# Compact 32x32 diagonal squares in two mixers, and attention steps that hold both key heads

## The chip, the cores and the metric

The kernel runs on one core of a Trainium2 chip. A core has a matrix engine (PE in the profile, with its weight loads listed apart as PEld), a vector engine (DVE), a scalar engine (ACT), a third elementwise engine (POOL) and a queue engine that issues transfers (SP). The metric is the time of one execution on the device in microseconds, lower is better, as the median of several runs.

## The reference

The program is two transformer-like blocks over 1024 tokens of width 1024, all in float32, one after the other. Three parts of it matter here.

1. Block one, sliding-window attention: 8 query heads of 64 share 2 key heads. Each of 8 query blocks of 128 tokens looks at its own and the preceding block, with a mask and one sink logit per head, as in `probs = softmax(concat([s, sink]))[..., :-1]`.
2. Block one, gated delta rule, 4 heads of 128: per chunk it needs the inverse of a unit lower triangular matrix, `T = triangular_solve(eye + L, eye)`, and then a recurrence over chunks.
3. Block two, an HGRN2 mixer of 6 heads of 128: per chunk the scores are `einsum('bhtk,bhsk,bhtsk->bhts', qb, kb, exp(diff))`, where `diff` is a difference of running sums for every feature k, and so the scores are no plain matrix product. A recurrence over chunks follows here too.

Around these stand projections, two MLPs of width 4096 and norms, which are most of the arithmetic.

## The kernel before, in words

Large products are split: a float32 operand is rounded to a high part and a rest (`split`, L191 and L192), and `acc` (L211 to L213) issues three single-pass matmuls of 128x512 for each tile. Small products run in plain float32. In the trace each plain float32 matmul stands as two matmul records, for instance 128 matmuls as 256 records; below, "record" means one of these.

The mixers work on half the sequence at a time, a tile being 128 partitions by 512 columns, that is four chunks of 128 tokens side by side.

**Attention** (`attn`, L634): one task per query block n and key head kv, 16 tasks. A task goes twice (jj) over two query heads: scores (L649 or L651, 64 rows of the array, those of head kv), mask (L654), maximum, exponential on ACT (L662), division (L668), yield, transposes (L673) and a copy (L675), yield, product with the values (L679, 64 columns of the array). One output tile is kept for the whole task, is copied out once (L682), and then sent by one transfer.

**Delta inverse** (`delta`, L723): X starts as the identity, and level l joins squares of side 2^l into squares of twice the side. Level 0 is elementwise (L776, L777). Levels 1 to 4 issue for each of the four chunks a product of the whole 128x128 L with the odd columns of X (L782), a transpose of X on DVE (L784), a masked copy (L785), a second product per chunk (L789) and a subtraction (L790). Everything that the mask removes was computed too. Levels 5 and 6 (L807, L815) already use blocks of 32 and 64. There are 4 heads by 2 halves, so 8 tasks.

**HGRN scores** (`hgrn`, L1174): the diagonal comes from a full product per chunk (L1181) times the identity; level 0 from one product with ones (L1192); levels 1 to 4 from a product per chunk of all keys with the odd queries (L1196), of which a predicated copy (L1197) keeps the masked part. Levels 5 and 6 use column blocks of 32 and 64 (L1202). There are 6 heads by 2 halves, so 12 tasks.

**What sets the order.** `weave` (L325) steps up to three tasks, one for each lane, in turn. After each round it advances a filler (projections and first output products) at a rate: RA while fewer than FA attention tasks have ended, then RB, then R1 when all have ended; R5 is the HGRN mixer's. Lane 0 takes only the first FA attention tasks, and then delta tasks. Each lane has its own two PSUM tiles (`axps(lane)`). The framework then plans the final order of instructions on each engine from dependencies, tile availability, modelled durations and the order in which the code issued them: an instruction whose inputs the plan has ready can go ahead of one that was issued earlier. On the chip, each engine's queue runs in the planned order.

Of the kernel before, what the change touches and what calls it, by code (L numbers as in the profile page):

```python
# [15 lines left out]
S = 1024  # L16
# [37 lines left out]
RA, RB, R1, R5 = 0.1, 0.2, 0.35, 0.9  # L54
FA, POOL_AT = 10, 2
# [6 lines left out]
def block_kernel(ctx: ExitStack, tc: tile.TileContext, A):  # L62
# [12 lines left out]
    const.tile([128, 64], F32, name="pad")  # L75
# [82 lines left out]
    def mask(l):  # L158

        a = cst("masks")[:, l * 64:(l + 1) * 64].rearrange("p (n b) -> p n b", b=1 << l)  # L160
        return a.unsqueeze(1).to_broadcast([128, 4, 64 >> l, 1 << l])
# [15 lines left out]

    def half4(t, l):

        return t[:, 0:256].rearrange("p (c n b) -> p c n b", c=4, b=1 << l)  # L180
# [339 lines left out]


# [99 lines left out]
    gh, gl = [wba[:, 0:32], wba[:, 32:64]]  # L621
    split(gg, gh, gl)
# [11 lines left out]
    def attn(lane, qr, kr, vT, n, kv):  # L634
# [4 lines left out]
        r = slice(kv * 64, kv * 64 + 64)  # L639
        am = cst("amask")[:, 256 - w:256].unsqueeze(1).to_broadcast([128, 2, w])  # L640
        po = axps(lane)
        for jj in range(2):
            ps = axps(lane)
            p3 = ps[:, :2 * w].rearrange("p (j k) -> p j k", j=2)
            for i in range(2):
                q = qr[2 * jj + i][n // 4][r, cs(n % 4)]
                if n % 4 == 0:
                    for b, m in enumerate(blocks):
                        PE.matmul(p3[:, i, cs(b)], q, kr[m // 4][r, cs(m % 4)], start=True, stop=True)  # L649
                else:  # L650
                    PE.matmul(p3[:, i], q, kr[n // 4][r, (n % 4 - 1) * 128:(n % 4 + 1) * 128], start=True, stop=True)  # L651
            e = td("ab"[jj], lane)
            e3 = e[:, :2 * w].rearrange("p (j k) -> p j k", j=2)
            V.tensor_tensor(e3, p3, am, ALU.add)  # L654
            yield
            m, nm, den, s2 = sm(2, "am"), sm(2, "an"), sm(2, "ad"), sm(2, "as")
            sk = small("sinks", kv * 4 + 2 * jj, 2)
            V.tensor_reduce(m, e3, AX.X, ALU.max)
            V.tensor_tensor(m, m, sk, ALU.max)
            V.tensor_scalar(nm, m, -1.0, None, ALU.mult)  # L660
            for i in range(2):
                SC.activation(e3[:, i], e3[:, i], ACTF.Exp, bias=nm[:, i:i + 1], accum_out=s2[:, i:i + 1])  # L662
            V.tensor_tensor(den, sk, m, ALU.subtract)
# [3 lines left out]
            for i in range(2):  # L667
                V.tensor_scalar(e3[:, i], e3[:, i], den[:, i:i + 1], None, ALU.mult)  # L668
            yield
            pp = axps(lane)  # L670
            for q in range(nb):
                for i in range(2):
                    PE.transpose(pp[:, cs(2 * q + i)], e3[:, i, cs(q)], ident)  # L673
            pT = td("tmp", lane)
            SC.copy(pT[:, :2 * w], pp[:, :2 * w])  # L675
            yield
            for q, m in enumerate(blocks):
                b = (m % 4) * 128 + kv * 64
                PE.matmul(po[r, jj * 256:jj * 256 + 256], vT[m // 4][:, b:b + 64],  # L679
                          pT[:, q * 256:q * 256 + 256], start=(q == 0), stop=(q == nb - 1))  # L680
        f = td("tmp", lane)
        SC.copy(f[r, :], po[r, :])  # L682
        mix["done"].update((n // 4, i) for i in range(4))
        nc.sync.dma_start(
            out=mix["d"][0:512, cs(n)].rearrange("(i q) t -> q i t", q=128)[r],
            in_=f[r, :].rearrange("p (i t) -> p i t", i=4),
        )
# [35 lines left out]
    def delta(lane, j, h, y, z):  # L723
# [49 lines left out]
        X = td("d", lane)  # L773
        Y = td("a", lane)
        G.tensor_copy(g4(X), b4(ident))
        V.tensor_tensor(half4(Y, 0), odd(U, 0, 4), mask(0), ALU.mult)  # L776
        V.tensor_tensor(odd(X, 0, 4), odd(X, 0, 4), half4(Y, 0), ALU.subtract)  # L777
        yield
        for l in range(1, 5):
            py = axps(lane)  # L780
            for c in range(4):
                PE.matmul(py[:, c * 64:c * 64 + 64], L[:, cs(c)], odd(X[:, cs(c)], l), start=True, stop=True)  # L782
            Y, T = td("a", lane), td("b", lane)
            V.transpose(T, X)  # L784
            V.tensor_tensor(half4(Y, l), half4(py, l), mask(l), ALU.mult)  # L785
            yield
            pz = axps(lane)
            for c in range(4):
                PE.matmul(pz[:, c * 64:c * 64 + 64], T[:, cs(c)], Y[:, c * 64:c * 64 + 64], start=True, stop=True)  # L789
            V.tensor_tensor(odd(X, l, 4), odd(X, l, 4), half4(pz, l), ALU.subtract)  # L790
            yield

        for l in range(5, 7):
# [4 lines left out]
            if l == 5:  # L798
                V.transpose(T, X)
# [5 lines left out]
            for c in range(4):  # L805
                for e, o in at:
                    PE.matmul(py[e, c * b:c * b + b], g4(L)[o, c, e], g4(X)[o, c, o], start=True, stop=True)  # L807
# [4 lines left out]
            for c in range(4):  # L812
                m = slice(c * b, c * b + b)
                for e, o in at:
                    PE.matmul(pz[e, m], g4(T)[e, c, e], Y[e, m], start=True, stop=True)  # L815
# [67 lines left out]
    def attn_task(lane, n, kv):  # L883
        yield from attn(lane, *qkv, n, kv)
        over[0] += 1

    def delta_task(lane, jh):

        while over[0] < (FA if lane == 0 else 2 * NC):
# [17 lines left out]
    tasks = [lambda lane, n=n, kv=kv: attn_task(lane, n, kv) for n in range(NC) for kv in range(2)]  # L907
    few = tasks[FA:]
    tasks += [lambda lane, jh=jh: delta_task(lane, jh) for jh in order]
    weave(tasks, fill, lambda: R1 if over[0] == 2 * NC else RB if over[0] >= FA else RA, few)  # L910
# [263 lines left out]
    def hgrn(lane, j, h, q, f, k, vT, g, direct):  # L1174


        sc = tx()[:, 0:H]

        ps = axps(lane)
        for c in range(4):  # L1180
            PE.matmul(ps[:, cs(c)], k[:, cs(c)], q[:, cs(c)], start=True, stop=True)  # L1181
        V.tensor_tensor(g4(sc), g4(ps), b4(ident), ALU.mult)
        yield
        V.tensor_tensor(q, q, f, ALU.mult)
        for l in range(7):
# [235 lines left out]
```

## Time and profile before

| what | value |
|---|---|
| median of 3 runs | 2673.6 us (2668.96 to 2673.8) |
| profiled execution, its own time | 2670.03 us |
| its span in the profile | 2667.9 us |
| PE busy | 2570.0 us, 96% |
| DVE busy | 1794.8 us, 67% |
| ACT busy | 971.1 us, 36% |
| POOL busy | 356.9 us, 13% |

The profiled execution's own time is 2.1 us longer than its span. Three stages concern the change: attention from about 137 us, with the first delta task from about 240 us; the other delta tasks up to about 590 us; and the HGRN mixer from about 1520 to 1960 us. The durations of neighbouring matmuls overlap in the profile, so what a matmul costs is read from the chain of waits, which gives each instruction the time by which it moved the end on.

### The profile page before, as it was taken

How to read it: one execution, taken by the hardware profiler on the slowest of the kernel's cores; microseconds unless marked ns; L12 is line 12 of the kernel's file. 1: busy time of each engine (PE TensorE's matmuls, PEld its weight loads, DVE VectorE, ACT ScalarE, POOL GpSimd, SP SyncE). 2: the span in 40 equal slices, each digit the busy share in tenths (PEclk: the TensorE clock that was granted, in tenths of full speed). 3: DMA queues.
4: the chain of work that ended last, by engine and by line, in shares of the span. 5: the costliest groups of instructions: out<-in, count | busy, mean ns of one | idle time of the engine just before them, and what ended most of it. 6: DMA issues, size and time to landing. Idle time of an engine off the chain costs nothing.

```text
span 2667.9 us, 34945 instructions
## 1 busy us (share of the span) xinstructions
PE 2570.0 (96%) x12814; PEld 2081.7 (78%) x12814; DVE 1794.8 (67%) x3289; ACT 971.1 (36%) x1568; POOL 356.9 (13%) x398
## 2 busy tenths in 40 slices
PE   6999999999899999999999999999988999999997
PEld 4766787877688888878877888888867888888886
DVE  8777789878987765465457643446589876654653
ACT  4477533314322245344333322222133222444441
POOL 5511112110000000000022343333200000000000
PEclk8999999999999999999999999999989999999998
DMA  5312111245644366445422411113455433665652
GB/s 199 95 52 68 41 37 52 94 148 183 206 157 133 127 229 227 166 152 196 151 78 69 160 56 40 44 34 105 152 181 191 155 131 131 214 210 195 220 195 77
DMA packets 161675, 357.00 MB, mean 134 GB/s; under 512 B 18272, under 2 KB 22752, under 8 KB 161504
## 3 DMA queue, kind: packets, MB, share of 16 engines
q1 hardware_dynamic: 156080, 345.84, 38.5%
q10 hardware_dynamic: 5424, 8.94, 1.0%
q8 instruction: 100, 1.64, 0.3%
q14 instruction: 71, 0.58, 0.1%
HBM read 282.35 MB, written 69.73 MB: 132 GB/s over the span
## 4 chain that ended last, share of the span: by engine, by line
PE 83%; DVE 9%; issue 4%; POOL 2%; DMA 1%; ACT 1%; POOLq 0%; SPq 0%; DVEq 0%; ACTq 0%
PE m L212 13%; PE m L213 13%; PE m L211 13%; PE x L213 10%; PE x L212 10%; PE x L211 10%; PE x L1196 1%; PE x L679 1%; PE x L789 1%; PE x L782 1%; DVE wl L192 1%; PE x L651 1%; DVE u L192 1%; PE x L1202 1%; PE x L673 1%
## 5 line engine op out<-in xcount | busy, mean ns | idle before, releaser
L211 PE MATMUL m<-u,wh 128*128 128x512 f32 x1668 | 671.8, 403 | 11.0 <-ACT wh L191 6.8
L213 PE MATMUL m<-u,wl 128*128 128x512 f32 x1668 | 665.4, 399 | 11.1 <-DVE wl L192 11.1
L212 PE MATMUL m<-u,wh 128*128 128x512 f32 x1668 | 666.9, 400 | 2.4 <-DVE u L192 1.2
L192 DVE TENSOR_TENSOR wl<-wr,wh 128x1024 fp32r<-128x1024 f32 (+2 forms) x265 | 328.0, 1238 | 296.5 <-ACT wh L191 283.0
L191 ACT CAST wh<-wr 128x1024 fp32r<-128x1024 f32 (+2 forms) x265 | 276.0, 1041 | 548.0 <-PE m L212 335.5
L213 PE MATMUL x<-u,wl 128*128 128x512 f32 x1020 | 397.9, 391 | 6.4 <-DVE wl L192 6.4
L212 PE MATMUL x<-u,wh 128*128 128x512 f32 x1020 | 398.5, 391 | 4.1 <-DVE u L192 4.1
L211 PE MATMUL x<-u,wh 128*128 128x512 f32 x1020 | 398.6, 392 | 2.4 <-ACT u L191 2.2
L211 PEld LDWEIGHTS m<-u,wh 128*128 128x128 f32 x1668 | 317.2, 190 | 80.7 <-ACT wh L191 7.3
L213 PEld LDWEIGHTS m<-u,wl 128*128 128x128 f32 x1668 | 317.2, 190 | 79.6 <-DVE wl L192 13.3
L212 PEld LDWEIGHTS m<-u,wh 128*128 128x128 f32 x1668 | 317.3, 190 | 73.6 <-issue 6.6
L213 PEld LDWEIGHTS x<-u,wl 128*128 128x128 f32 x1020 | 192.3, 189 | 47.6 <-DVE wl L192 7.7
L212 PEld LDWEIGHTS x<-u,wh 128*128 128x128 f32 x1020 | 192.1, 188 | 45.9 <-DVE u L192 5.4
L211 PEld LDWEIGHTS x<-u,wh 128*128 128x128 f32 x1020 | 192.2, 188 | 44.9 <-ACT u L191 3.5
L191 ACT CAST u<-f 128x512 fp32r<-128x512 f32 x198 | 122.1, 620 | 187.6 <-PE x L212 73.8
L192 DVE TENSOR_TENSOR u<-f,u 128x512 fp32r<-128x512 f32 x174 | 123.4, 709 | 95.0 <-PE x L212 50.9
L191 ACT CAST wh<-y 128x512 fp32r<-128x512 f32 x91 | 55.1, 621 | 218.9 <-PE x L212 131.3
L192 POOL TENSOR_TENSOR u<-f,u 128x512 fp32r<-128x512 f32 x24 | 35.6, 1481 | 609.2 <-ACT u L191 608.4
L192 DVE TENSOR_TENSOR u<-r,u 128x512 fp32r<-128x512 f32 x128 | 88.1, 688 | 5.8 <-ACT u L191 5.8
L191 ACT CAST u<-r 128x512 fp32r<-128x512 f32 x128 | 79.2, 619 | 11.6 <-DMA r<-hid 8.8
L192 DVE TENSOR_TENSOR wl<-y,wh 128x512 fp32r<-128x512 f32 x91 | 61.7, 682 | 0.0
L248 DVE TENSOR_TENSOR ac<-ac,sq 128x512 f32<-128x512 f32 x70 | 53.7, 767 | 9.5 <-ACT sq L247 8.7
(742 smaller groups left out, 3714.1 us busy)
## 6 DMA issues: line engine op xcount, KB each, us to landing
wr<-in_w_down SPq DMA_DIRECT2D x128, 512.0 KB, 4.0
wr<-in_w_in SPq DMA_DIRECT2D x75, 512.0 KB, 3.2
r<-hid SPq DMA_DIRECT2D x128, 256.0 KB, 4.0
f<-hid SPq DMA_DIRECT2D x128, 256.0 KB, 3.3
y<-in_w_up SPq DMA_DIRECT2D x85, 256.0 KB, 3.2
hid<-f SPq DMA_DIRECT2D x52, 256.0 KB, 2.0
wr<-in_w_up SPq DMA_DIRECT2D x20, 512.0 KB, 4.0
hid<-sq SPq DMA_DIRECT2D x32, 256.0 KB, 3.1
```

What stands on the lines that cost most here:

```text
L191: SC.copy(hi, src)
L192: eng.tensor_tensor(lo, src, hi.bitcast(F32), ALU.subtract)
L211: PE.matmul(ps, whi[:, s], xh, start=(first and k == 0), stop=False)
L212: PE.matmul(ps, whi[:, s], xl, start=False, stop=False)
L213: PE.matmul(ps, wlo[:, s], xh, start=False, stop=(last and k == len(x) - 1))
L248: V.tensor_tensor(a, a, sq, ALU.add)
L651: PE.matmul(p3[:, i], q, kr[n // 4][r, (n % 4 - 1) * 128:(n % 4 + 1) * 128], start=True, stop=True)
L673: PE.transpose(pp[:, cs(2 * q + i)], e3[:, i, cs(q)], ident)
L679: PE.matmul(po[r, jj * 256:jj * 256 + 256], vT[m // 4][:, b:b + 64], pT[:, q * 256:q * 256 + 256], start=(q == 0), stop=(q == nb - 1))
L782: PE.matmul(py[:, c * 64:c * 64 + 64], L[:, cs(c)], odd(X[:, cs(c)], l), start=True, stop=True)
L789: PE.matmul(pz[:, c * 64:c * 64 + 64], T[:, cs(c)], Y[:, c * 64:c * 64 + 64], start=True, stop=True)
L1196: PE.matmul(ps[:, c * 64:c * 64 + 64], k[:, cs(c)], odd(q[:, cs(c)], l), start=True, stop=True)
```

## The change

1. **Delta inverse, levels 0 to 4.** X lives in a compact tile `Xc` of 128x128: the four 32x32 squares on the diagonal of a chunk stand under each other in 32 columns, and the four chunks side by side. Each product of a level is 16 matmuls of 32 rows by 32 columns by 16, one for each chunk and square, square i using row group i and column group i of the array. The DVE operations shrink from 512 or 256 columns to 128 or 64; level 0's masked product becomes four instructions, one for each square. After level 4 a zeroed X is filled by four ACT copies. Level 5 reads the compact tile.
2. **HGRN scores.** The diagonal product and levels 0 to 4 become 16 matmuls each of 128 rows by 32 columns, by 32 (diagonal) or 16, in the four column groups, into a compact tile `Sc`. Level 0 no longer has a product with ones. `sc` is zeroed by POOL, and four ACT copies put the squares in place after level 4. At level 5 the two column blocks of a chunk are issued in turn, and all copies follow.
3. **Attention.** One task per query block holds both key heads: 8 tasks. In each of its two passes the scores of the two heads are issued in turn, into two PSUM tiles, from the upper and the lower 64 rows; the small softmax operations work on four columns in place of two; the division is one DVE operation for each head; the products with the values are issued in turn into the upper and the lower 64 partitions of one tile, which is copied out and sent in each pass.
4. RA, RB and FA are scaled to the halved number of tasks. Two small tables (`cmasks`, `identc`) are made by twelve POOL copies at the start.

The diff, cut; of the attention function the new lines are shown, and the old ones stand in the listing above:

```diff
-RA, RB, R1, R5 = 0.1, 0.2, 0.35, 0.9
-FA, POOL_AT = 10, 2
+RA, RB, R1, R5 = 0.2, 0.4, 0.35, 0.9
+FA, POOL_AT = 5, 2
...
-    def mask(l):
-        a = cst("masks")[:, l * 64:(l + 1) * 64].rearrange("p (n b) -> p n b", b=1 << l)
-        return a.unsqueeze(1).to_broadcast([128, 4, 64 >> l, 1 << l])
+    cmask4 = const.tile([128, 16], F32, name="cmask4")
+    def dg(i):
+        return slice(32 * i, 32 * i + 32)
+    def cmask(l, b=None):
+        t = cmask4 if l == 4 else cmasks[:, l * 16:l * 16 + 16]
+        if b is None:
+            return t.unsqueeze(1).to_broadcast([128, 4, 16])
+        return t.rearrange("p (n b) -> p n b", b=b).unsqueeze(1).to_broadcast([128, 4, 16 // b, b])
+    DIAG = [(c, dg(i), slice(c * 128 + 32 * i, c * 128 + 32 * i + 32)) for c in range(4) for i in range(4)]
+    def cmasks_in():
+        for i in range(4):
+            m = cst("masks")[dg(i), :].rearrange("p (l n) -> p l n", l=5)[:, :, 16 * i:16 * i + 16]
+            G.tensor_copy(cmasks[dg(i), :].rearrange("p (l n) -> p l n", l=4), m[:, 0:4])
+            G.tensor_copy(cmask4[dg(i), :], m[:, 4])
...
+    cmasks_in()
+    identc = wba[:, 64:96].bitcast(F32)
+    for i in range(4):
+        G.tensor_copy(wba[dg(i), 64:96], ident[dg(i), dg(i)])
...
-    def attn(lane, qr, kr, vT, n, kv):
+    def attn(lane, qr, kr, vT, n):
         blocks = [n] if n == 0 else [n - 1, n]
         nb = len(blocks)
         w = nb * 128
+        rs = [slice(0, 64), slice(64, 128)]
         am = cst("amask")[:, 256 - w:256].unsqueeze(1).to_broadcast([128, 2, w])
         for jj in range(2):
+            ps = [axps(lane), axps(lane)]
+            p3 = [p[:, :2 * w].rearrange("p (j k) -> p j k", j=2) for p in ps]
             for i in range(2):
+                q = qr[2 * jj + i][n // 4]
                 if n % 4 == 0:
                     for b, m in enumerate(blocks):
+                        for kv, r in enumerate(rs):
+                            PE.matmul(p3[kv][:, i, cs(b)], q[r, cs(n % 4)], kr[m // 4][r, cs(m % 4)], start=True, stop=True)
                 else:
+                    for kv, r in enumerate(rs):
+                        PE.matmul(p3[kv][:, i], q[r, cs(n % 4)], kr[n // 4][r, (n % 4 - 1) * 128:(n % 4 + 1) * 128], start=True, stop=True)
+            es = [td("ab"[kv], lane)[:, :2 * w].rearrange("p (j k) -> p j k", j=2) for kv in range(2)]
+            for kv in range(2):
+                V.tensor_tensor(es[kv], p3[kv], am, ALU.add)
             yield
+            m, nm, den, s2 = [sm(4, t) for t in ("am", "an", "ad", "as")]
+            two = lambda t, kv: t[:, 2 * kv:2 * kv + 2]
+            sk = small("sinks", 0, 8).rearrange("p (v j) -> p v j", v=2)[:, :, 2 * jj:2 * jj + 2]
+            d2 = lambda t: t.rearrange("p (v j) -> p v j", v=2)
+            for kv in range(2):
+                V.tensor_reduce(two(m, kv), es[kv], AX.X, ALU.max)
+            V.tensor_tensor(d2(m), d2(m), sk, ALU.max)
             V.tensor_scalar(nm, m, -1.0, None, ALU.mult)
+            for kv in range(2):
+                for i in range(2):
+                    k = 2 * kv + i
+                    SC.activation(es[kv][:, i], es[kv][:, i], ACTF.Exp, bias=nm[:, k:k + 1], accum_out=s2[:, k:k + 1])
+            V.tensor_tensor(d2(den), sk, d2(m), ALU.subtract)
             SC.activation(den, den, ACTF.Exp)
             V.tensor_tensor(den, den, s2, ALU.add)
             V.reciprocal(den, den)
+            for kv in range(2):
+                V.tensor_tensor(es[kv], es[kv], two(den, kv).unsqueeze(2).to_broadcast([128, 2, w]), ALU.mult)
             yield
+            pT = []
+            for kv in range(2):
+                pp = axps(lane)
+                for q in range(nb):
+                    for i in range(2):
+                        PE.transpose(pp[:, cs(2 * q + i)], es[kv][:, i, cs(q)], ident)
+                t = td("tmp", lane)
+                SC.copy(t[:, :2 * w], pp[:, :2 * w])
+                pT.append(t)
             yield
+            po = axps(lane)
             for q, m in enumerate(blocks):
+                for kv, r in enumerate(rs):
+                    b = (m % 4) * 128 + kv * 64
+                    PE.matmul(po[r, 0:256], vT[m // 4][:, b:b + 64], pT[kv][:, q * 256:q * 256 + 256],
+                              start=(q == 0), stop=(q == nb - 1))
+            f = td("tmp", lane)[:, 0:256]
+            SC.copy(f, po[:, 0:256])
+            nc.sync.dma_start(
+                out=mix["d"][256 * jj:256 * jj + 256, cs(n)].rearrange("(i q) t -> q i t", q=128),
+                in_=f.rearrange("p (i t) -> p i t", i=2),
+            )
         mix["done"].update((n // 4, i) for i in range(4))
     tails = const.tile([128, 36], F32, name="tails")
...
-        X = td("d", lane)
-        Y = td("a", lane)
-        G.tensor_copy(g4(X), b4(ident))
-        V.tensor_tensor(half4(Y, 0), odd(U, 0, 4), mask(0), ALU.mult)
-        V.tensor_tensor(odd(X, 0, 4), odd(X, 0, 4), half4(Y, 0), ALU.subtract)
+        Xc, Y = td("g", lane)[:, 0:128], td("a", lane)[:, 0:64]
+        y4 = lambda t: t[:, 0:64].rearrange("p (c n) -> p c n", c=4)
+        G.tensor_copy(g4(Xc), identc.unsqueeze(1).to_broadcast([128, 4, 32]))
+        for i in range(4):
+            V.tensor_tensor(y4(Y)[dg(i)], g4(U)[dg(i), :, 32 * i + 1:32 * i + 32:2], cmask(0)[dg(i)], ALU.mult)
+        V.tensor_tensor(odd(Xc, 0), odd(Xc, 0), Y.unsqueeze(2), ALU.subtract)
         yield
+        blocks = [(c, dg(i), slice(c * 128 + 32 * i, c * 128 + 32 * i + 32), slice(c * 16, c * 16 + 16)) for c in range(4) for i in range(4)]
         for l in range(1, 5):
             py = axps(lane)
-            for c in range(4):
-                PE.matmul(py[:, c * 64:c * 64 + 64], L[:, cs(c)], odd(X[:, cs(c)], l), start=True, stop=True)
-            Y, T = td("a", lane), td("b", lane)
-            V.transpose(T, X)
-            V.tensor_tensor(half4(Y, l), half4(py, l), mask(l), ALU.mult)
+            for c, p, m, n in blocks:
+                PE.matmul(py[p, n], L[p, m], odd(Xc[p, dg(c)], l), start=True, stop=True)
+            Y, T = td("a", lane)[:, 0:64], td("b", lane)[:, 0:128]
+            V.transpose(T, Xc)
+            V.tensor_tensor(y4(Y), y4(py), cmask(l), ALU.mult)
             yield
             pz = axps(lane)
-            for c in range(4):
-                PE.matmul(pz[:, c * 64:c * 64 + 64], T[:, cs(c)], Y[:, c * 64:c * 64 + 64], start=True, stop=True)
-            V.tensor_tensor(odd(X, l, 4), odd(X, l, 4), half4(pz, l), ALU.subtract)
+            for c, p, m, n in blocks:
+                PE.matmul(pz[p, n], T[p, dg(c)], Y[p, n], start=True, stop=True)
+            V.tensor_tensor(odd(Xc, l), odd(Xc, l), pz[:, 0:64].rearrange("p (n b) -> p n b", b=1 << l), ALU.subtract)
             yield
+        X = td("d", lane)
+        G.memset(X, 0.0)
+        for i in range(4):
+            SC.copy(g4(X)[dg(i), :, dg(i)], Xc[dg(i), :].rearrange("p (c n) -> p c n", c=4))
         for l in range(5, 7):
             b = 1 << l
...
-                V.transpose(T, X)
+                V.transpose(T[:, 0:128], Xc)
-                    PE.matmul(py[e, c * b:c * b + b], g4(L)[o, c, e], g4(X)[o, c, o], start=True, stop=True)
+                    x = Xc[o, dg(c)] if l == 5 else g4(X)[o, c, o]
+                    PE.matmul(py[e, c * b:c * b + b], g4(L)[o, c, e], x, start=True, stop=True)
-                    PE.matmul(pz[e, m], g4(T)[e, c, e], Y[e, m], start=True, stop=True)
+                    PE.matmul(pz[e, m], T[e, m] if l == 5 else g4(T)[e, c, e], Y[e, m], start=True, stop=True)
...
-    tasks = [lambda lane, n=n, kv=kv: attn_task(lane, n, kv) for n in range(NC) for kv in range(2)]
+    tasks = [lambda lane, n=n: attn_task(lane, n) for n in range(NC)]
-    weave(tasks, fill, lambda: R1 if over[0] == 2 * NC else RB if over[0] >= FA else RA, few)
+    weave(tasks, fill, lambda: R1 if over[0] == NC else RB if over[0] >= FA else RA, few)
...
         sc = tx()[:, 0:H]
+        G.memset(sc, 0.0)
+        Sc = tl(ph, f"S{lane}", 1, 128)
         ps = axps(lane)
-        for c in range(4):
-            PE.matmul(ps[:, cs(c)], k[:, cs(c)], q[:, cs(c)], start=True, stop=True)
-        V.tensor_tensor(g4(sc), g4(ps), b4(ident), ALU.mult)
+        for c, p, m in DIAG:
+            PE.matmul(ps[p, dg(c)], k[:, m], q[:, m], start=True, stop=True)
+        V.tensor_tensor(g4(Sc), g4(ps[:, 0:128]), identc.unsqueeze(1).to_broadcast([128, 4, 32]), ALU.mult)
         yield
         V.tensor_tensor(q, q, f, ALU.mult)
         for l in range(7):
             b = 1 << l
             ps = axps(lane)
-            if l == 0:
-                p = tt("r")[:, 0:256]
-                pairs = [t.rearrange("p (n x) -> p n x", x=2) for t in (q, k)]
-                V.tensor_tensor(p, pairs[0][:, :, 1], pairs[1][:, :, 0], ALU.mult)
-                PE.matmul(ps[:, 0:256], ones, p, start=True, stop=True)
-                V.copy_predicated(odd(sc, l, 4), mask(l).bitcast(I32), half4(ps, l))
-            elif l < 5:
-                for c in range(4):
-                    PE.matmul(ps[:, c * 64:c * 64 + 64], k[:, cs(c)], odd(q[:, cs(c)], l), start=True, stop=True)
-                V.copy_predicated(odd(sc, l, 4), mask(l).bitcast(I32), half4(ps, l))
+            if l < 5:
+                for c, p, m in DIAG:
+                    PE.matmul(ps[p, c * 16:c * 16 + 16], k[:, m], odd(q[:, m], l), start=True, stop=True)
+                V.copy_predicated(odd(Sc, l, 4), cmask(l, b).bitcast(I32), ps[:, 0:64].rearrange("p (c n b) -> p c n b", c=4, b=b))
+                if l == 4:
+                    for i in range(4):
+                        SC.copy(g4(sc)[dg(i), :, dg(i)], Sc[dg(i), :].rearrange("p (c n) -> p c n", c=4))
             else:
                 at = [(slice(i, i + b), slice(i + b, i + 2 * b)) for i in range(0, 128, 2 * b)]
+                for c in range(4):
+                    for e, o in at:
+                        PE.matmul(ps[e, c * b:c * b + b], g4(k)[:, c, e], g4(q)[:, c, o], start=True, stop=True)
                 for e, o in at:
-                    for c in range(4):
-                        PE.matmul(ps[e, c * b:c * b + b], g4(k)[:, c, e], g4(q)[:, c, o], start=True, stop=True)
                     SC.copy(g4(sc)[e, :, o], ps[e, :4 * b].rearrange("p (c n) -> p c n", c=4))
             yield
             nb = H // (2 * b)
```

## Rows read from the trace of the kernel before

**Rows 1.** The page: busy time by engine, and the chain that ended last by engine.
```profile
PE 2570.0 (96%) x12814; PEld 2081.7 (78%) x12814; DVE 1794.8 (67%) x3289; ACT 971.1 (36%) x1568; POOL 356.9 (13%) x398
...
PE 83%; DVE 9%; issue 4%; POOL 2%; DMA 1%; ACT 1%; POOLq 0%; SPq 0%; DVEq 0%; ACTq 0%
```

**Rows 2.** Busy time by stretch: PE, PEld, DVE, ACT, POOL, PE clock, DMA share, GB/s.
```profile
137.00:240.00 103.00, 102.18 (x469) 68.48 (x468) 78.60 (x234) 75.76 (x183) 11.68 (x20) 1.00 0.18 58
...
310.00:590.00 280.00, 269.77 (x2011) 225.16 (x2010) 236.24 (x602) 90.50 (x137) 55.92 (x57) 1.00 0.22 76
1520.00:1960.00 440.00, 431.26 (x2514) 361.58 (x2514) 227.60 (x498) 110.20 (x192) 150.19 (x211) 1.00 0.22 77
```

**Rows 3.** Matmul groups by line and shape: busy us, mean ns, idle before.
```profile
L782 PE MATMUL x<-d,c 128*128 128x64 f32 x256 | 32.9, 270 | 0.1
...
L1196 PE MATMUL x<-e,g 128*128 128x64 f32 x64 | 8.9, 276 | 0.0
...
L1202 PE MATMUL x<-e,g 128*32 128x32 f32 x32 | 1.8, 199 | 0.0
```

**Rows 4.** Chain of waits, a delta level: start us, us moved on, what.
```profile
338.28 0.84 PE x L782 x8
339.12 0.28 PE m L212
```

**Rows 5.** Chain of waits around level 5 of the delta inverse.
```profile
286.73 0.37 PE x L807 x16
287.10 0.43 PE m L212
287.53 0.23 PE m L213
...
288.68 0.17 PE x L815 x2
...
289.95 0.36 PE x L815 x14
```

**Rows 6.** Chain of waits, sums in four column groups, 128 columns each.
```profile
242.13 0.36 PE x L232 x8
```

**Rows 7.** Chain of waits, HGRN diagonal product, a level, and level 0.
```profile
1521.13 1.78 PE x L1181 x16
...
1528.85 0.84 PE x L1196 x8
1529.68 0.49 PE x L1192 x2
```

**Rows 8.** Chain of waits, one column block of HGRN level 5.
```profile
1562.09 0.37 PE x L1202 x8
```

**Rows 9.** Chain of waits, attention: scores of two lanes, of one, values, scores, exit.
```profile
137.36 0.65 PE x L649 x8
...
169.32 1.01 PE x L679 x4
170.33 1.06 PE x L651 x4
...
173.45 0.43 PE m L212
...
196.04 1.08 PE x L649 x8
```

**Rows 10.** Matmuls in order of time in the attention stage.
```profile
154.72 0.27 PE L673 MATMUL x<-consts,b 128*128 128x128 f32 x1
154.74 0.48 PE L213 MATMUL m<-u,wl 128*128 128x512 f32 x1
```

**Rows 11.** DVE and ACT groups by line and shape: busy us, mean ns, idle before.
```profile
L784 DVE STREAM_TRANSPOSE b<-d 128x512 f32<-128x512 f32 x32 | 22.5, 703 | 0.1
...
L675 ACT COPY tmp<-x 128x512 f32<-128x512 f32 x28 | 16.3, 582 | 15.8 <-PE x L673 15.6
...
L1203 ACT COPY x<-x 32x128 f32<-32x128 f32 x24 | 6.1, 252 | 26.7 <-PE x L1202 26.6
```

More of the change, by code (lines that the diff above doesn't have):

```diff
@@ L73, in block_kernel @@
     ps_ = ctx.enter_context(tc.tile_pool(name="ps", bufs=1))
-    const.tile([128, 64], F32, name="pad")
+    cmasks = const.tile([128, 64], F32, name="cmasks")
     psm = ctx.enter_context(tc.tile_pool(name="psm", bufs=2, space=bass.MemoryType.PSUM))
@@ L176, in odd @@
         return t.rearrange("p (c n x b) -> p c n x b", c=n, x=2, b=1 << l)[:, :, :, 1]
-    def half4(t, l):
-        return t[:, 0:256].rearrange("p (c n b) -> p c n b", c=4, b=1 << l)
     def hs(h):
@@ L638, in attn @@
         w = nb * 128
-        r = slice(kv * 64, kv * 64 + 64)
+        rs = [slice(0, 64), slice(64, 128)]
         am = cst("amask")[:, 256 - w:256].unsqueeze(1).to_broadcast([128, 2, w])
-        po = axps(lane)
         for jj in range(2):
-            ps = axps(lane)
-            p3 = ps[:, :2 * w].rearrange("p (j k) -> p j k", j=2)
+            ps = [axps(lane), axps(lane)]
+            p3 = [p[:, :2 * w].rearrange("p (j k) -> p j k", j=2) for p in ps]
             for i in range(2):
-                q = qr[2 * jj + i][n // 4][r, cs(n % 4)]
+                q = qr[2 * jj + i][n // 4]
@@ L647, in attn @@
                 if n % 4 == 0:
                     for b, m in enumerate(blocks):
-                        PE.matmul(p3[:, i, cs(b)], q, kr[m // 4][r, cs(m % 4)], start=True, stop=True)
-                else:
[L651 to L654, printed above, removed]
-            yield
@@ L656, in attn @@
[L656 to L659, printed above, removed]
-            V.tensor_scalar(nm, m, -1.0, None, ALU.mult)
-            for i in range(2):
-                SC.activation(e3[:, i], e3[:, i], ACTF.Exp, bias=nm[:, i:i + 1], accum_out=s2[:, i:i + 1])
-            V.tensor_tensor(den, sk, m, ALU.subtract)
+                        for kv, r in enumerate(rs):
+                            PE.matmul(p3[kv][:, i, cs(b)], q[r, cs(n % 4)], kr[m // 4][r, cs(m % 4)], start=True, stop=True)
+                else:
+                    for kv, r in enumerate(rs):
+                        PE.matmul(p3[kv][:, i], q[r, cs(n % 4)], kr[n // 4][r, (n % 4 - 1) * 128:(n % 4 + 1) * 128], start=True, stop=True)
@@ L666, in attn @@
             V.reciprocal(den, den)
-            for i in range(2):
-                V.tensor_scalar(e3[:, i], e3[:, i], den[:, i:i + 1], None, ALU.mult)
+            for kv in range(2):
+                V.tensor_tensor(es[kv], es[kv], two(den, kv).unsqueeze(2).to_broadcast([128, 2, w]), ALU.mult)
             yield
[L670 to L675, printed above, removed]
+            pT = []
[7 more added lines that the diff above has]
+                pT.append(t)
             yield
+            po = axps(lane)
             for q, m in enumerate(blocks):
[L678 to L682, printed above, removed]
+                for kv, r in enumerate(rs):
[8 more added lines that the diff above has]
+            )
         mix["done"].update((n // 4, i) for i in range(4))
[L684 to L687, printed above, removed]
     tails = const.tile([128, 36], F32, name="tails")
@@ L881, in block_kernel, with attn_task @@
     over = [0]
-    def attn_task(lane, n, kv):
-        yield from attn(lane, *qkv, n, kv)
+    def attn_task(lane, n):
+        yield from attn(lane, *qkv, n)
         over[0] += 1
     def delta_task(lane, jh):
-        while over[0] < (FA if lane == 0 else 2 * NC):
+        while over[0] < (FA if lane == 0 else NC):
             yield
```

## The prediction

> **What bounds the kernel now.** I read the page first: PE is busy 96% of the span, and 83% of the chain that ended last is PE's own work; apart from PE's own weight loads, which lie beside its matmuls, nothing passes 67% [rows 1]. Then the busy time by stretch, since the change touches only the two mixers: in all three stretches PE is busy 96 to 99% of the time at a granted clock of 1.00 (the 2.4 GHz level), while DVE has 24 us free of 103 in the attention stretch, 44 of 280 in the delta stretch and 212 of 440 in HGRN's [rows 2]. So time is won where PE's queue gets shorter. A few microseconds of waiting are in there too: 10.2 us without PE in the delta stretch and 8.7 in HGRN's. What a matmul costs I take from the chain of waits, because group means overlap.
>
> The counts come from the code and agree with the groups: L782 stands 256 times for 8 tasks, 4 levels and 4 chunks, two records a matmul [rows 3]; L789 stands 256 times too, and L1196 in six groups of 64.
>
> **Prices of small squares.** A delta step of 8 full-array records moves the end on by 0.84 us, and the next large matmul by 0.28 in place of 0.23, so 0.89 a step [rows 4, 5]. Of small records I take three facts. First, a run of small squares has an entry and an exit: 2 records of L815 cost 0.17, and the large matmul behind 16 records of L807 costs 0.43, which is 0.20 more than the one after it [rows 5]. Second, spacing: 14 records of L815 cost 0.19 more than 2, so 0.016 each, with two column groups in turn [rows 5]; 8 records of L1202 in one column group cost 0.37, and without an entry of 0.15 that is 0.031 each [rows 8]. Two groups halve the spacing. Third, four column groups do work side by side: 8 records of L232 with 128 columns, two to each column group, cost 0.36 [rows 6], where records of 128 columns one after another cost 0.11 each (L1181, 1.78 for 16 [rows 7]). From these I estimate 0.008 for a record with four groups in turn. A run of 32 is then 0.15 + 31 x 0.008 + 0.20 = 0.60 us.
>
> The bounds: at the pace of two groups (0.016) a run costs 0.85, at that of one (0.031) 1.31. The nearest row in shape is L815, in count of groups L232; I take 0.60, because spacing halved from one group to two and rows 6 show four at work.
>
> The spacing of 0.016 us is a mean over 12 records of different column groups [rows 5]. The Trainium skill, "TensorE: Matmul & The Clock Gate", in "Wait — 56ns, not 53.3ns?", says that start-to-start never falls below about 25 ns however few columns are moved. The trace disagrees with it, at 16 ns. By that rule a run would cost an estimated 1.13 us, dearer than the step that it replaces.
>
> **Delta inverse, levels 1 to 4.** Removed: 8 tasks x 4 levels x 2 = 64 steps of 0.89 = 57.0 us. Added: 64 runs of 0.60 = 38.4. Gain 18.6 (bounds: gain 2.6 at 0.016, loss 26.8 at 0.031). Level 5 has the same matmuls as before. The DVE work beside it shrinks: the transpose of 512 columns (703 ns [rows 11]) becomes one of 128, the masked copies go from 256 columns to 64; level 0 becomes four small instructions. It is not on PE's path, so I cost it at nothing, and it makes each step ready earlier. New beside it: a zeroing of X on POOL, busy 56 of 280 there [rows 2], and four ACT copies a task of 32 by 128, at 252 ns from L1203 [rows 11], 8 us in all on an engine with 190 us free. Both are due only before level 5's result is put into X; without that cover a task would wait about 1 us, 8 in all.
>
> **HGRN scores.** A task now pays 0.89 for the diagonal, 0.49 for level 0, 4 x 0.89 for levels 1 to 4 [rows 4, 7], and twice 0.37 + 0.20 for level 5 [rows 8, 5]: 6.08, for 12 tasks 73.0 us. Afterwards it pays six runs of 0.60, and for level 5 one run of 16 at two groups, 0.15 + 15 x 0.016 + 0.20 = 0.59: 4.19, or 50.3. Gain 22.7 (bounds: gain 4.7, loss 35). DVE loses work again. POOL gets one zeroing a task and ACT four copies (12 us over the stage); they have 290 and 330 us free [rows 2]. The zeroing waits for a free `x` tile, and POOL's products for the next level are queued behind it; but the tile's last reader is issued well before, so I cost that at nothing.
>
> **Attention.** Two heads use different halves of the array. The trace has this once: at 137.36 two lanes' scores meet, 8 records in 0.65 us, where 8 of one head take 1.08 [rows 9]. If all heads ran so, every second group would go with its exit. Scores: 12 x (1.06 + 0.20) for the six blocks with records of 256 columns, 2 x (1.08 + 0.20) for block 4 and 2 x 0.84 for block 0, whose groups are half as long: 19.4 us. Values: 14 x (1.01 + 0.20) and 2 x 0.78 for block 0: 18.5. Together 38 us, the one end. The other end is nothing: as many groups as before.
>
> What decides is whether the plan keeps the heads together. It puts a matmul in as soon as its own input is due: a single transpose stands between large matmuls [rows 10]. The two heads' probabilities leave ACT 0.58 us apart (L675 [rows 11]), and the four value records of the first take 1.01; so I take half of each head's records as overlapped: a pair costs 1.5 x 1.01 + 0.20 = 1.72 in place of 2 x 1.21, which is 9.8 us for 14 pairs and 10.5 with block 0. For the scores the change adds a wait: a lane has two PSUM tiles, and the second head's must first hold the preceding value product and be copied out, while before one output tile stayed for the whole task and scores followed values at once (169.32 and 170.33 [rows 9]). So I count only the first pass of each of three lanes, 3.5 us. Queued behind that wait on PE are large matmuls, which the plan moves ahead of it; DVE's mask step of the second head waits. In sum 14 us. The transfers to `mix` stay 16, of the same total size; DVE and ACT do about the same work in fewer instructions.
>
> **What is added elsewhere.** The plan can cut a run in two: L815's 16 came as 2 and 14, with two entries and exits [rows 5], 0.35 a cut. With one in ten of the 64 delta runs that is 2 us. Less PE work leaves less to lie beside the chains: 3 us, between nothing and 19 (the idle time of both stretches once more). Twelve small POOL copies at the start: 1 us, up to 3 at ACT's 0.25 each.
>
> Sum: -18.6 - 22.7 - 14 + 2 + 3 + 1 = -49.3 us. The profiled execution's own time is 2670.0 (2.1 over its span), which gives **2621 us**. That execution lies 3.6 us under the median of the runs and within their spread of 4.8.
>
> **The rivals.**
> 1. *The heads stay together throughout.* For it: the 0.65 of rows 9. Against: the 0.58 us between the heads and the lost output tile. It takes 38 in place of 14: 2597 us. It goes no lower, because in the attention stretch DVE and ACT are already at 79 and 76 of 103 us [rows 2].
> 2. *The squares go only as fast as two groups*, 0.016 a record. For it: that is the only long run of squares in the trace. Gains 2.6 + 4.7 + 14, less 6: 2655 us.
> 3. *Slower: small records pass one by one*, whichever group they use, so that four groups give no more than two or even lose: the place is the 136 new runs, the price their spacing s. They cost 136 x (0.35 + 31 x s) and 7.1 for level 5 of HGRN, against 57.0 + 73.0 now; with attention and the additions the change breaks even at s = 0.020 us. Halfway between one group's 0.031 and two groups' 0.016, at 0.024, they cost 156, so 2670 + 26 - 14 + 6 = 2688 us. For it: no run in the trace alternates four groups more than twice. Against it: 0.016 with only two [rows 5], and rows 6. With the 25 ns of the Trainium skill's page named above it would be an estimated 2692 us.
> 4. *The change does not do what it says in attention*: the plan separates all heads, or cover is lost to the full 19 us. 2635 to 2651 us.
>
> **How the numbers follow.** The forecast (2605 to 2640) gets 0.52, rival 1 0.20, rival 2 0.13, rival 4 beyond the forecast's range 0.06, rival 3 0.07, and 0.02 remain for a result within 0.2%, about what a measurement of this kernel can tell from no change. Rival 3 is taken to end inside that limit a seventh of the time. So faster 0.91, same 0.03, slower 0.06. The range leaves out rival 3, part of rival 1 and the last of rival 4: 2592 to 2656.
>
> **What would show it.** Right: the runs of 32 at the new lines of the inverse and the scores move the chain on by 0.35 to 0.45 us, and large matmuls behind them by 0.43; the delta stretch is about 20 us shorter and HGRN's about 23; DVE's busy time falls; values stand as runs of 8 records of about 1.4 us, scores mostly as two runs of 4 with large matmuls between. Wrong: runs of 32 of 0.65 or more (rival 2), of 0.9 or more (rival 3), score runs of 8 in about 1.08 throughout (rival 1), or PE idle in the mixers beyond 30 us in sum (rival 4).

## The result, and the profile after

The changed kernel takes **2612.4 us** (median of 4 runs, 2610.6 to 2615.6) where the kernel before, run beside it, takes 2672.0 (2669.0 to 2673.8): a ratio of 0.9779 [0.9762, 0.9796], 59.5 us less. The forecast was 2621 (2592 to 2656). The profiled execution of after took 2615.6 us, 54.4 less than that of before, and the forecast had been made from that one.

First the page of after, busy time by engine and the chain by engine, to be held against [rows 1].

```profile
PE 2503.3 (96%) x16150; PEld 2010.0 (77%) x16150; DVE 1742.7 (67%) x3189; ACT 987.3 (38%) x1632; POOL 377.6 (14%) x430
...
PE 66%; issue 3%; DVE 3%; POOL 1%; ACT 1%; DMA 0%; POOLq 0%; DVEq 0%; ACTq 0%
```

PE has 3336 records more and is busy 67 us less, DVE 52 us less; PE is still busy 96% of the span and still the bound. The chain's shares add up to only 74%, since in this trace it is not followed back through the delta stretch; PE's share is not comparable with before's 83%.

The stages by stretch, first before and then after (columns as in [rows 2]): attention and delta, the MLPs between, and HGRN.

```profile
137.30:590.60 453.30, 442.25 (x2898) 344.60 (x2898) 365.56 (x985) 209.44 (x414) 76.88 (x90) 1.00 0.21 69
590.60:1521.00 930.40, 904.50 (x3977) 736.83 (x3976) 622.14 (x936) 341.09 (x502) 56.52 (x44) 0.99 0.48 161
1521.00:1945.50 424.50, 418.54 (x2462) 351.82 (x2460) 216.47 (x470) 102.79 (x181) 147.70 (x210) 1.00 0.21 73
```

```profile
136.50:551.80 415.30, 398.49 (x4416) 304.21 (x4416) 330.67 (x894) 211.49 (x430) 83.60 (x98) 0.99 0.22 71
551.80:1493.60 941.80, 915.25 (x3995) 745.02 (x3993) 624.30 (x938) 340.86 (x502) 58.95 (x47) 0.98 0.49 161
1493.60:1891.00 397.40, 388.19 (x4262) 314.91 (x4261) 197.30 (x458) 116.96 (x229) 153.14 (x219) 1.00 0.24 78
```

Attention and delta got 38.0 us shorter, HGRN 27.1, and the middle, whose code did not change, 11.4 longer. PE's idle time (stretch less busy) went from 11.1 to 16.8 us in the first stage and from 6.0 to 9.2 in the third. Of the middle's 11.4 us about 4 are 18 large matmuls of the filler that used to stand inside the delta stretch and now come after its last task. Most of the rest goes with the granted clock, whose mean there is 0.98 in place of 0.99: it stood at 0.5 for 34 us of this stretch in place of 17, and the 512-column matmuls that started in those times took 14.7 us beyond their usual time in place of 6.8.

The new runs in the chain of waits in HGRN (columns as in [rows 4]); before, a level stood there as one piece of 0.84.

```profile
1572.05 0.22 PE x L1274 x2
1572.27 0.38 PE x L1231 x32
1572.64 0.43 PE m L223
1573.07 0.23 PE m L224
...
1578.31 0.47 PE x L433 x4
1578.78 0.38 PE x L1231 x32
1579.15 0.30 PE x L1222 x19
1579.45 0.43 PE m L223
1579.88 0.23 PE m L224
```

A run of 32 moves the end on by 0.38, and the large matmul behind it by 0.43, 0.20 more than the next: 0.58 in all. Two runs of different tasks also stand side by side, and then share one entry and one exit. In the delta stretch the order on PE by time shows the same (start, busy us of the group, line, shape, count):

```profile
288.83 0.45 PE L845 MATMUL x<-d,c 64*64 64x64 f32 x5
289.21 0.44 PE L815 MATMUL x<-g,c 32*32 32x16 f32 x32
289.49 0.45 PE L822 MATMUL x<-a,b 32*32 32x16 f32 x32
289.87 0.50 PE L223 MATMUL m<-u,wh 128*128 128x512 f32 x1
```

From the start of L815's 32 to that of L822's lie 0.28 us. The start times of the records in such a run, in ns from its first, read 0, 7, 13, 20, then 53, 59, 66, 73, and from there four more every 32 ns: four records, one in each column group, start 7 ns apart, and a group is used again after 32 ns.

The small work on DVE and ACT (columns as in [rows 11]):

```profile
L817 DVE STREAM_TRANSPOSE b<-g 128x128 f32<-128x128 f32 x32 | 9.6, 303 | 0.4
L1235 ACT COPY x<-S 32x128 f32<-32x128 f32 x48 | 14.2, 296 | 11.1 <-DVE S L1232 9.4 <-POOL tmp L1249 1.1
L828 ACT COPY d<-g 32x128 f32<-32x128 f32 x32 | 9.4, 295 | 13.4 <-DVE g L823 13.1
```

The transpose fell from 703 to 303 ns, and the new copies cost 296 ns each, 24 us on ACT, beside PE's work.

### The profile page after: what moved, and what is told of

It reads as the page before. It is cut to its first block, busy times and chain, and to the rows that moved or that the text cites. A ratio compares the mean times of both kernels' runs of the same rounds, so it can differ in the third digit from the quotient of the medians.

```text
span 2613.2 us, 41652 instructions
## 1 busy us (share of the span) xinstructions
PE 2503.3 (96%) x16150; PEld 2010.0 (77%) x16150; DVE 1742.7 (67%) x3189; ACT 987.3 (38%) x1632; POOL 377.6 (14%) x430
## 4 chain that ended last, share of the span: by engine, by line
PE 66%; issue 3%; DVE 3%; POOL 1%; ACT 1%; DMA 0%; POOLq 0%; DVEq 0%; ACTq 0%
PE x L225 10%; PE m L223 10%; PE x L224 10%; PE x L223 10%; PE m L225 10%; PE m L224 10%; PE x L1231 1%; POOL u L204 0%; PE x L1240 0%; PE x L1272 0%; PE x L1258 0%; PE x L1274 0%; DVE wl L204 0%; DVE u L204 0%; DMA f<-hid 0%
```

## The experiments

Each kernel ran beside runs of the kernel before on the same chip; differences below are against those, by the ratio, and their 95% intervals reach 2.5 to 5.5 us to either side. Differences from the control are between the medians where nothing else is said. "The control" is the changed kernel run once more, beside the sixth to eighth experiment: 2612.35 us, ratio 0.9765 [0.9752, 0.9779].

> The changed kernel once more, as the measure for the runs beside it: 2612 us, within 4.

**1. Attention alone.** The kernel before with the new `attn` and the scaled rates, the inverse and HGRN as they were.

```diff
+RA, RB, R1, R5 = 0.2, 0.4, 0.35, 0.9
+FA, POOL_AT = 5, 2
+    def attn(lane, qr, kr, vT, n):
```

> Only the attention of the change (both heads in a task, RA, RB, FA scaled); delta inverse and HGRN as before. Theory A, PE's queue sets the end and the parts add up: the score and value groups cost 18.6 us less in the trace of the changed kernel, a few of which go to new idle time, so 12 to 18 us less than before. Rival B, the gain comes from the shorter DVE work of the inverse and the scores: attention's DVE work is nearly the same, so 0 to 4 us less. Rival C, the parts take each other's cover: 18 us or more less here, and the three parts alone add to 70 us or more.

2658.8 us, ratio 0.9942 [0.993, 0.9955]: 15.5 us less. What the scaled rates do by themselves no run shows; the trace of the change has 16.2 us less PE work in attention, which leaves them little. The attention and delta stretch:

```profile
136.50:578.10 441.60, 424.73 (x2882) 341.42 (x2882) 358.70 (x870) 199.65 (x396) 80.38 (x90) 0.98 0.21 67
```

**2. The delta inverse alone.** Only `delta`'s levels 0 to 4 and the step into level 5.

```diff
+            for c, p, m, n in blocks:
+                PE.matmul(py[p, n], L[p, m], odd(Xc[p, dg(c)], l), start=True, stop=True)
```

> Only the delta inverse of the change; attention and HGRN as before. Theory A: 22.8 us less in PE's queue by the trace of the changed kernel, 17 to 22 us less in time. Rival B: more than its PE saving, 25 us or more. Rival C: 22 us or more, and the three parts alone add to 70 us or more.

2660.3 us, ratio 0.9942 [0.9928, 0.9955]: 15.5 us less, somewhat under what was expected. The stretch:

```profile
138.00:570.40 432.40, 417.86 (x4418) 310.78 (x4418) 340.20 (x1007) 218.32 (x446) 79.63 (x98) 0.99 0.22 69
```

It is 20.9 us shorter, and PE waits 14.5 us in it, 3.5 more than before; the middle grew by 6.

**3. HGRN alone.**

```diff
+            for c, p, m in DIAG:
+                PE.matmul(ps[p, dg(c)], k[:, m], q[:, m], start=True, stop=True)
```

> Only the HGRN scores of the change; attention and delta inverse as before. Theory A: 31.4 us less in PE's queue by the trace of the changed kernel, 25 to 30 us less in time. Rival B: DVE has half of this stretch free, so its shorter work gives nothing beyond PE's: the same. Rival C: 30 us or more.

2648.6 us, ratio 0.9898 [0.9885, 0.9912]: 27.3 us less. The delta stretch, with the code of before, and HGRN's:

```profile
137.90:595.40 457.50, 447.45 (x2898) 349.24 (x2898) 364.99 (x983) 209.61 (x414) 76.50 (x90) 0.99 0.22 67
1527.60:1924.70 397.10, 388.17 (x4261) 314.73 (x4261) 197.35 (x458) 116.97 (x229) 153.25 (x219) 1.00 0.25 78
```

HGRN's stretch is that of the whole change to within 0.3 us. The three parts alone make 58.3 us, the whole 59.1 and 62.8 in its two comparisons: they add, as far as intervals of about 3.5 us to either side of each can tell, and the 70 us or more of rival C lie outside them. The first line also shows how far an unchanged stretch wanders: 457.5 us against 453.3, at a mean clock of 0.99.

**4. One column group after the other.** The same matmuls, the four squares of one column group issued next to each other.

```diff
-    DIAG = [... for c in range(4) for i in range(4)]
+    DIAG = [... for i in range(4) for c in range(4)]
...
-        blocks = [... for c in range(4) for i in range(4)]
+        blocks = [... for i in range(4) for c in range(4)]
```

> The changed kernel, but the 16 matmuls of every square product are issued group by group (all four chunks of square 0, then of square 1, ...), so that neighbours in the queue use the same column group. Same matmuls, same sizes. Theory A, neighbours in different column groups lie side by side, and in the same group they follow at 0.031 us: 136 runs cost 31 x 0.023 = 0.71 us more each, 97 us, so about 2709 us, slower than before. Rival: the array takes small matmuls out of order or paces them by instruction, so that the order does not matter: 2612 us, within 5.

2674.1 us, ratio 1.000 [0.9991, 1.001]: the whole gain is gone, 62 us above the control. The chain in this kernel:

```profile
1692.04 0.38 PE x L1240 x16
1692.42 0.69 PE x L1231 x32
1693.11 0.43 PE m L223
1693.54 0.23 PE m L224
```

```profile
287.33 0.23 PE m L225
287.56 0.81 PE x L815 x32
288.37 0.60 PE m L223
288.97 0.43 PE m L224
```

Within a group the records stand 32 ns apart, but where one group's squares end and the next one's begin they overlap, and so a run spans 0.70 us from its first start to its last (0.26 in the change). 136 runs x 0.44 = 60 us, near the 62 measured. That the two agree so closely is partly chance, since two smaller terms partly cancel: in the profiles, this kernel has 133 us at the lower clock where the control has 81, which goes with 14 us more in the 512-column matmuls that started in them, and PE is idle for 8 us less. The expected 97 took no overlap at the seams. The large matmuls of 0.60 and 0.43 behind the second piece stand in a stretch at the lower clock.

**5. Two column groups in turn.**

```diff
-    DIAG = [... for c in range(4) for i in range(4)]
+    DIAG = [... for u in (0, 2) for c in range(4) for i in (u, u + 1)]
```

(and `blocks` in the same way)

> The change with its 16 matmuls of a run issued in another order: squares 0 and 1 of all four chunks first, then squares 2 and 3, so that only two column groups alternate at a time. The same matmuls, the same results. Theory A (PE's queue is the bound, and a record's price is 0.031 us divided by the column groups in turn): 136 runs of 32 records at 0.016 in place of 0.008 cost 136 x 31 x 0.008 = 34 us more, so 2612 + 34 = 2646 us, with runs of 32 at 0.60 to 0.65 us. Rival D (the pace is set by the engine's issue, not by the groups): no more than 5 us off 2612. Rival G (two groups already run as fast as four where each lasts only 16 columns): below 2625.

2621.4 us, ratio 0.9808 [0.9788, 0.9829]: 9 us above the control by the medians, 11.5 by the ratios. The time is below rival G's line and far below theory A's 34. The chain:

```profile
285.40 0.23 PE m L225
285.64 0.52 PE x L815 x30
286.15 0.43 PE m L223
286.58 0.23 PE m L224
```

A run spans 0.41 us from its first start to its last, 0.013 a record and not 0.016, because where the pairs of groups change the next pair starts beside the last. Inside a pair the pace is theory A's: the starts read 0, 6, 52, 59, 84, 90, 115, 122 ns, two records every 32 ns, and the second pair's first record starts at 160, long before the first pair's last at about 250. So rival G's number came true, but not its reason. Summed over all runs and what they delay, PE's queue is 15 us longer than in the change, which goes with 9 to 11.5 in the time.

**6. The level runs of HGRN issued twice**, into the same place: 60 runs of 32 records more.

```diff
-                for c, p, m in DIAG:
+                for c, p, m in DIAG + DIAG:
```

> The changed kernel with each of the 60 runs of HGRN levels 0 to 4 issued twice over, the second copy of 16 matmuls overwriting the first with the same numbers. No new switch of the array's shape, no new DVE, ACT or POOL work. Theory A (PE's queue is the end, four column groups give 0.008 us a record): 60 x 32 x 0.008 = 15 us more. Rival B (these stretches are paced by the chains through DVE and POOL, PE has slack): 0 to 3 us more. Rival D (the run's cost is its records and not its entry and exit, about 0.6 us a run): 30 us or more.

2628.8 us, ratio 0.983 [0.9816, 0.9843]: 16.5 us above the control, and HGRN's stretch went from 397.4 to about 412.

```profile
1490.00:1902.00 412.00, 403.49 (x6138) 330.52 (x6125) 194.24 (x458) 116.87 (x230) 154.80 (x219) 1.00 0.24 77
```

1920 records at 0.008 are 15.4: PE's queue is the bound in this stretch, and that is what a record costs.

**7. Attention's heads issued one after the other** in place of in turn, within each group of scores and of values.

```diff
-            for q, m in enumerate(blocks):
-                for kv, r in enumerate(rs):
+            for kv, r in enumerate(rs):
+                for q, m in enumerate(blocks):
```

> The changed kernel, but in attention all score matmuls of the first key head are issued before those of the second, and likewise the value products; everything else the same. Theory A (neighbours from different heads lie side by side on the array, and the plan keeps part of them together): 8 to 14 us more than the changed kernel. Rival E (the plan separates the heads anyway, and attention won by having half as many groups to enter and leave): within 3 us of it.

2611.7 us, ratio 0.9768 [0.9755, 0.9781]: no difference. A group of values in the changed kernel and in this one, by time:

```profile
157.15 0.70 PE L670 MATMUL x<-c,e 64*128 64x256 f32 x2
157.68 0.59 PE L670 MATMUL x<-c,g 64*128 64x256 f32 x2
158.20 1.08 PE L708 MATMUL x<-tmp,d 128*64 128x256 f32 x8
159.22 0.70 PE L670 MATMUL x<-c,e 64*128 64x256 f32 x2
159.75 0.59 PE L670 MATMUL x<-c,g 64*128 64x256 f32 x2
```

```profile
159.87 1.09 PE L707 MATMUL x<-tmp,d 128*64 128x256 f32 x8
160.89 0.48 PE L669 MATMUL x<-c,e 64*128 64x256 f32 x1
```

Eight records of two heads take 1.09 us even where the code issues four of one head and then four of the other: their starts read 0, 13, 266, 280 ns and so on, so the second head's records, four further back, began beside the first head's. The seams of experiment 4 look the same: there the first record of the next column group starts right behind the fifth of eight (148, then 154 ns), with three of its predecessors yet to start. Both would fit a queue in which up to three waiting records can be passed; the trace lists records by their start, so the order in the queue itself is not shown. In these traces the order inside such a group of eight does not matter; whether the other head's records are ready at all does. The scores show that: at 157.15 and 159.22 one head's four records stand alone, at 1.05 us, as in [rows 9].

**8. Another tile for `gt`.** In the changed kernel PE waits longest in the first stage for a POOL product (in all, times, longest, us):

```profile
PE x L777 <- POOL tmp L776: 8.2, 12, 2.0
PE x L433 <- POOL tmp L429: 3.5, 5, 1.3
```

```diff
-            gt = td("tmp", lane, F32R)
+            gt = td("cd"[i], lane, F32R)
```

> The changed kernel, but the two decay tiles that POOL prepares at the start of a delta task (L776) go into the lane's c and d tiles in place of the tmp tiles, which hold the squares until the sums have read them; so POOL can start sooner. Theory F (PE's 8.2 us of waiting at L777 for POOL, 4.3 in the kernel before, is time on the path): 4 to 8 us less than the changed kernel. Rival: the plan only moves the wait to another place: within 2 us.

2611.5 us, ratio 0.9768 [0.9754, 0.9781]: nothing. The wait is gone from the list, and others stand there:

```profile
PE x L433 <- POOL tmp L429: 4.1, 5, 1.9
PE x L799 <- DVE b L788: 2.6, 2, 2.4
PE x L699 <- DVE a L692: 2.0, 2, 1.5
PE x L845 <- DVE g L823: 1.4, 1, 1.4
```

PE's idle time in the stretch is 16.1 us (16.8 in the change's profile, 17.9 in the control's).

**9. The second head's copy on DVE.**

```diff
-                SC.copy(t[:, :2 * w], pp[:, :2 * w])
+                (V.tensor_copy if kv else SC.copy)(t[:, :2 * w], pp[:, :2 * w])
```

> The change with the second head's copy of transposed probabilities moved from ACT to DVE, so that the copies of the two heads need no longer queue one behind the other on ACT, and the second head's value records are ready sooner. Theory A (the values' overlap is limited by the 0.6 us between the two copies): half of the value runs not yet full turn into runs of 8 records, 4 to 7 us less than the change, 2605 to 2608 us, and mean times of value records below 127 ns. Rival H (the overlap is set by what the plan puts between, or DVE, already at three quarters of its time there, gives the gain back): within 3 us of the change, 2609 to 2615.

2615.0 us, ratio 0.9776 [0.9762, 0.9791]: no gain, as rival H had it; value records stand eight together in 4 groups, where the change has 6. The stretch:

```profile
139.50:558.50 419.00, 400.35 (x4416) 304.59 (x4416) 340.81 (x910) 202.28 (x412) 82.97 (x98) 0.99 0.22 71
```

DVE took over 10 us and the two heads' values did not meet more often; PE waits 18.7 us. The experiment did not bring about what it was to test: the copies of a pair end 0.78 us apart (median of 14) where they end 0.49 apart in the change, since a copy takes 0.69 us on DVE and starts later. So it tells that this kernel is no faster, and not what a shorter distance would give. Neither this nor the eighth gave a version faster than the change.

## Why the prediction was right, step by step

Each part's PE work below is summed over the trace: by how much every record of its matmuls moved PE's end on, and what the next matmul of another part took beyond its usual time. HGRN's level 6, which is not in the forecast, costs the same before and after.

| part | before | after | gain | forecast | time, part alone |
|---|---|---|---|---|---|
| delta inverse | 59.0 | 35.5 | 23.5 | 18.6 | 15.5 |
| HGRN scores | 81.9 | 50.1 | 31.8 | 22.7 | 27.3 |
| attention | 68.6 | 52.4 | 16.2 | 14 | 15.5 |
| sum | 209.5 | 138.0 | 71.5 | 55.3 | 58.3 |

The expectations of experiments 1 to 3 count 18.6, 22.8 and 31.4; for attention that takes the entry of a group that stands right behind another one twice. The busy time of the stretches agrees with the table: PE's fell by 43.8 us in the first, about 4 of them the filler that moved out, and by 30.4 in HGRN's.

**The price of a run held.** Forecast 0.60 us from an entry of 0.15, 0.008 a record and an exit of 0.20; measured 0.58 for a run alone where the step before was put at 0.89 [rows 4, 5], and 0.55 as the mean of delta's 64 (35.5 / 64) and 0.50 of HGRN's 72 (36.1 / 72), since some share an entry and an exit. The fear of cut runs did not come true as a loss: the plan cuts some and joins more (13 pairs and 3 threes in HGRN, 10 pairs in delta). Rival 3's case, that small records pass one by one, exists, but as an order of issue: experiment 4 is it, and its end is the time of before. Of the rule cited in the prediction, from the Trainium skill's "TensorE: Matmul & The Clock Gate", section "Wait — 56ns, not 53.3ns?" (about 25 ns from start to start at least), these runs show that it can't hold between column groups: 7 ns there, and 32 within one group.

**Rival 2's pace did not appear, and its price stands.** Four groups in turn cost 0.0085 a record. Two groups in turn cost the 0.016 of L815 [rows 5] inside a pair, though those records move 32 columns where these move 16; that experiment 5 lost 9 to 11.5 us to the control and not 34 comes first from the overlap at the one seam of each run, which leaves 0.15 us a run, 20 in all; 15 of these show in PE's queue.

**Both mixers cost more before and less after than forecast.** Of HGRN's 9.1 us beyond the forecast, 3.4 are L1196's 48 groups (46.1 us in place of 42.7) and 7.1 the new runs (36.1 in place of 43.2, by joining); the other terms take back about 1. Delta's 4.9 are 2.0 from the groups removed and 2.9 from joined runs. One row per kind was taken for all of its kind, and joining was not in the sum.

**Attention came out near its size, but not in the form foretold.** Each counted by itself, values went from 36.5 to 25.3 us, 11.2 against 10.5 forecast, and scores from 37.5 to 30.1, 7.4 against 3.5; together, with no entry taken twice, it is 16.2 against 14. The forecast took half of each head's value records as overlapped, in runs of 8 of about 1.4 us. Only 6 of the 14 full pairs stand as 8, most of them in 1.01 us; the other 8 stand as 2 records of the first head (0.58) and then 6 (1.01). The mean of the two forms is close to the 1.72 a pair of the forecast, and that is luck. Half of L670's runs are of 4 records (9 of 18), as foretold from the lost output tile; but in others heads or lanes meet, beyond the first pass. Why the values do not meet more often stays open: the 0.49 us between the two copies may be the reason, and experiment 9 lengthened it.

**The cover was the term most undersized.** Forecast +3 us of PE idle; measured +9 in the two mixers (+10 in the control), +12 over the span. Experiment 8 shows that it is no single wait: with the largest removed, others filled its place. So 71.5 us less work gave 59.5 after idle time, and 54.4 in the profiled pair. The 5.1 between go with the lower clock: the granted clock is at 0.5 for 95 us of after's profile and 74 of before's, and the 512-column matmuls that started in those times took 28.8 us beyond their usual time in place of 22.0, 6.8 more. In the control it is 81 us and 23.8, and its time lies 62 under before's. Whether the change brings such episodes on stays open. The kernel of experiment 3 has 95 us too, 14 of them in a stretch whose code it did not touch; but the mean granted clock is 0.983 to 0.989 in the executions of before, 0.981 to 0.985 in the eight of the changed kernel, and 0.975 to 0.979 in all ten of experiment 4, the same matmuls in another order.

So the forecast was 8.6 us high. Gains of work that were 16.2 too small and the 3 us for cuts and the start, which cost nothing that shows, make 19.2; 9 of cover and 5.1 with the clock go the other way; and the profiled execution of after lies 3.2 over its median. The mechanism and the price of a run were right; that the total came within 9 us is partly luck, since errors of 19 and 14 us stood against each other.

## What to carry to other kernels

Where a mask throws away most of a product, issue the blocks that remain as small squares, with neighbours in the queue in different column groups: the order alone was worth 62 us here. Count an entry and an exit (0.13 and 0.20 us) for each run and let runs stand side by side. And when PE's queue gets shorter, price the cover: of 72 us of matmul work removed, 12 came back as waiting, and removing the longest wait gave nothing, as others took its place.

## What the runs showed of the hardware

- A column group took a new record of 16 columns every 32 ns, the time of one of 32 columns too (0.031 us [rows 8]), and four groups took one each within that time, 7 ns apart: 0.0085 us a record with four in turn, 0.013 with two, 0.023 with one (0.26, 0.41 and 0.70 us over 31 steps), the last two helped by overlap where groups change.
- Records of different column groups overlapped though the code does not issue them next to each other: value records of the second head, issued four places back, started 13 ns after the first head's, and in experiment 4 the next group's first record started when three of the group before had not.
- A run of small squares delayed the large matmul behind it by 0.20 us in every order and length seen: 0.43 in place of 0.23 behind a run of 32 in four, two or one groups, behind two runs joined, and behind the doubled runs of experiment 6.
